# One 512-column product per high weight tile in the gate and up projections of a streaming encoder

## The chip, the core and the metric

The kernel runs on one core of a Trainium2 chip. The core's engines work side by side and meet at semaphores only: TensorE (PE in the profile, its weight loads PEld), VectorE (DVE), ScalarE (ACT), GpSimd (POOL) and SyncE (SP), which issues the loads. The metric is the time of one execution on the device in microseconds (us), as the median of several runs.

## The reference

Two layers run over a sequence of 256 tokens with 1024 features. Each layer is a gated feed-forward half step, a mixing step with three groups of heads, and a second gated feed-forward half step, each followed by a layer norm. The change is in the feed-forward part, of which there are four:

```
def swiglu(x, w_gu, w_down):
    gate, up = jnp.split(x @ w_gu, 2, axis=-1)
    return (jax.nn.silu(gate) * up) @ w_down

x = layer_norm(ALPHA * x + 0.5 * swiglu(x, ffn1_w_gu[l], ffn1_w_down[l]), ln1_g[l], ln1_b[l])
...
x = layer_norm(ALPHA * x + 0.5 * swiglu(x, ffn2_w_gu[l], ffn2_w_down[l]), ln3_g[l], ln3_b[l])
```

`w_gu` is 1024 by 5632 (2816 gate columns, then 2816 up columns), `w_down` 2816 by 1024, all float32.

## The kernel before

**Parts.** Every float32 operand of a large product is split in two: a high part rounded to the format that TensorE multiplies in one pass (fp32r), and a low part, the difference. A product is the sum of three: high by high, high by low, low by high. ScalarE writes the high part of a weight piece (`split_from`, L232) and VectorE the low part (L233), both in pieces of 128x512. The tokens `x` stand as two blocks of 128 tokens; `make_xT` transposes and splits them into the tiles `xh` and `xl`, each [128, 2 blocks, 4 k, 128 tokens], two pairs of them for the 8 slices of 128 features (`k`).

**Units.** A stage is a list of units of 128x1024 weight values. `load` brings a unit's raw weights into one of 5 buffers, `split` makes its two parts in one of 7 pairs of buffers (`wh`, `wl`), and `job` issues its products. `prepare` keeps up to 7 units split ahead of the products, and 5 loaded ahead of the splits. The instructions of an engine run in the order in which the builder's scheduler lays them down.

**Gate and up.** The 2816 columns are cut into 11 chunks of 256, each with its 256 gate columns and 256 up columns. The first 2 chunks of a feed-forward part are done block by block, because the second block's tokens arrive later. The other 9 (the ones with `both` set, 36 units) take both blocks at once, with the weights as the stationary operand and 256 token columns moving. A unit of these holds 2 slices `k` of all 512 columns of its chunk, so a chunk has 4 units and each unit 4 tiles of 128 columns:

```
for n, (a, x) in enumerate(((wh[:, s], xh), (wh[:, s], xl), (wl[:, s], xh))):
    self.nc.tensor.matmul(
        o, lhsT=a, rhs=x, start=k == 0 and n == 0 and i % 2 == 0, stop=end and n == 2,
```

That is three products of 256 columns for each tile and `k` (L295), added up in one half of a PSUM bank; the moving operand takes 128 columns from each block, in two pieces 512 values apart. A chunk uses two of the four banks of the pool `ps`. When it is done, `after_gu2` takes SiLU of the gate half on ScalarE (L447), multiplies by the up half on VectorE (L448), and splits the result into `hT`, the stationary operand of the down projection.

**Down.** The 22 units of `w_down` follow, per block, with `hT` as the stationary operand and 512 weight columns moving (`mm3`, L221, L222, L228, tile `po`). The input projection of the mixing step (`win`) uses the same code as gate and up for seven of its groups, with three products of 256 columns.

Of the kernel before, what the change touches and what calls it, by code (L numbers as in the profile page):

```python
# [11 lines left out]
F32R = mybir.dt.float32r  # L12
AF = mybir.ActivationFunctionType
# [4 lines left out]
P = 128  # L18
SEQ = 256
D = 1024  # L20
DFF = 2816
# [9 lines left out]
TSC = 2  # L31
# [60 lines left out]
class Kernel:  # L92
    def __init__(self, ctx, tc, a, out):
        self.tc, self.nc, self.a, self.out = tc, tc.nc, a, out
        pool = lambda name, bufs, **kw: ctx.enter_context(tc.tile_pool(name=name, bufs=bufs, **kw))
        self.const = pool("const", 1)
        self.raw_p = pool("raw", NRAW)
        self.wh_p = pool("wh", NW)
        self.wl_p = pool("wl", NW)
        self.xt_p = pool("xt", 4)  # L100
        self.big_p = pool("big", NBIG)
        self.w_p = pool("w", NHALF)
        self.h_p = pool("h", NH)
        self.s_p = pool("s", NS)
        self.gb_p = pool("gb", 1)
        psum = dict(space=bass.MemoryType.PSUM)
        self.ps_p = pool("ps", 4, **psum)
        self.aux_p = pool("aux", 4, **psum)
        self.n = 0
# [165 lines left out]
    def job(self, u, b):  # L275


        wh, wl = u["wh"], u["wl"]
        if u["kind"] in ("gu", "win"):
            width, ks = u["width"], u["ks"]  # L280
            g = u["group"]
            if u["part"] == 0:
                g["ps", b] = [self.ps("ps") for _ in range(len(u["tiles"]) // 2 if u["both"] else 1)]
            banks = g["ps", b]
            last = u["part"] == KD // ks - 1
            if u["both"]:
                for i, c0 in enumerate(u["tiles"]):
                    o = banks[i // 2][:, 256 * (i % 2) : 256 * (i % 2) + 256]
                    for kk in range(ks):
                        k = u["part"] * ks + kk  # L290
                        xh, xl = (t[:, :, k % 4, :] for t in self.xT[k // 4])
                        s = slice(kk * width + c0, kk * width + c0 + P)
                        end = last and kk == ks - 1
                        for n, (a, x) in enumerate(((wh[:, s], xh), (wh[:, s], xl), (wl[:, s], xh))):
                            self.nc.tensor.matmul(  # L295
                                o, lhsT=a, rhs=x, start=k == 0 and n == 0 and i % 2 == 0, stop=end and n == 2,
                                skip_group_check=True,
                            )
                        self.clock += 3 * 256 / 2400
                    if i < len(u["tiles"]) - 1:  # L300
                        self.step()
                if last:
                    self.spawn(u["then"](u, *banks))
                return
            ps = banks[0][:, :width]
            for kk in range(ks):
                k = u["part"] * ks + kk
                xh, xl = (t[:, b, k % 4, :] for t in self.xT[k // 4])
                s = slice(kk * width, (kk + 1) * width)
                self.mm3([ps], xh, xl, [(wh[:, s], wl[:, s])], k == 0, k == KD - 1)  # L310
            if last:
                self.spawn(u["then"](u, b, ps))
        else:
            if u["first"]:
                self.po[b] = [self.ps("po") for _ in range(2)]
            parts = self.hT if u["kind"] == "down" else self.mT
            t, kk = parts[u["k"] // 2, b], u["k"] % 2
            ws = [(wh[:, n * 512 : (n + 1) * 512], wl[:, n * 512 : (n + 1) * 512]) for n in range(2)]
            po = self.po[b]
            self.mm3(po, t[:, 0, kk, :], t[:, 1, kk, :], ws, u["first"], u["last"])  # L320
# [71 lines left out]

    def make_xT(self, b, seg):

        x = self.x[b]
        if b == 0:
            self.next_xT = []
        for n in range(2):
            ps = self.aux(b, "xps")
            self.transposes([x[:, (4 * n + k) * P : (4 * n + k + 1) * P] for k in range(4)], ps)  # L400
            if b == 0:
                self.next_xT.append(
                    [self.xt_p.tile([P, 2, 4, P], F32R, tag="xt", name=self.name(s)) for s in ("xh", "xl")]
                )
            hi, lo = self.next_xT[n]
            self.split_from(ps.rearrange("p (k t) -> p k t", k=4), hi[:, b], lo[:, b])
            yield 0.7
            self.xT = self.next_xT
            self.xready.add((seg, n, b))
# [28 lines left out]
        yield 0.8  # L438
        self.hT[u["c"], b] = g["hT"][:, b]

    def after_gu2(self, u, *banks):

        nc = self.nc
        tmp = self.big([2, 2, 256], "sghh")
        sg, hh = tmp[:, 0], tmp[:, 1]
        for j, ps in enumerate(banks):
            nc.scalar.activation(sg[:, j], ps[:, 0:256], AF.Silu)  # L447
            nc.vector.tensor_mul(hh[:, j], ps[:, 256:512], sg[:, j])  # L448
        t = self.big([2, 2, 2, P], "hT", F32R)
        self.split_from(hh.rearrange("p j (b t) -> p b j t", b=2), t[:, :, 0], t[:, :, 1])  # L450
        yield 1.0
        for b in range(2):
            self.hT[u["c"], b] = t[:, b]


    def after_win(self, u, *rest):
# [578 lines left out]
    def segments(self):  # L1035
        a = self.a
        segs = []

        def ffn(l, f):
            seg = len(segs)  # L1040
            last = l == L - 1 and f == 2
            units = []
            for c in range(NCH):
                group = {}
                both = c >= TSC
                for part in range(4):
                    units.append(
                        dict(kind="gu", w=a[f"ffn{f}_w_gu"][l], c=c, part=part, width=512, ks=2, group=group,
                             cols=((c * 256, 256), (DFF + c * 256, 256)), both=both, tiles=(0, 256, 128, 384),
                             then=self.after_gu2 if both else self.after_gu)  # L1050
                    )
# [146 lines left out]
```

## Time and profile before

| | us |
|---|---|
| median of 3 runs | 1108.71 (1108.1 to 1108.74) |
| the profiled execution | 1108.88 |
| its span, first to last instruction | 1107.1 |
| mean granted clock of TensorE in it | 0.992 of full speed |

| engine | busy, us | share of the span | instructions |
|---|---|---|---|
| PE | 1069.0 | 97% | 7549 |
| PEld | 961.6 | 87% | 7549 |
| DVE | 707.0 | 64% | 1351 |
| ACT | 555.8 | 50% | 1104 |
| POOL | 42.0 | 4% | 51 |

A matmul's duration in the profile includes its way through the array, during which the next one has begun; what a matmul costs in a row of them is the distance from its start to the next start. The chain of waits counts the time so. In it, the products of line L295 have 43% of the span, those of the down projection (`po`, L221, L222, L228) 21%.

### The profile page before, as it was taken

The numbers are of one execution on the slowest core, as the hardware profiler recorded it, in microseconds if no ns is written. First come the engines' busy times: TensorE is split into PE (matmuls) and PEld (weight loads), VectorE is DVE, ScalarE is ACT, GpSimd is POOL, SyncE is SP. The second block draws the span as 40 slices with busy tenths as digits, with TensorE's granted clock in tenths as the row PEclk, the third lists the DMA queues.
The fourth block names the chain that finished last, engine by engine and source line by source line (L and its number), as shares of the span: only waits on it lengthen the run. The fifth ranks groups of instructions, "written<-read, shape, count | busy, mean of one in ns | idle before, by whom it ended". The sixth has DMA issues, their size and how long they took to land.

```text
span 1107.1 us, 19618 instructions
## 1 busy us (share of the span) xinstructions
PE 1069.0 (97%) x7549; PEld 961.6 (87%) x7549; DVE 707.0 (64%) x1351; ACT 555.8 (50%) x1104; POOL 42.0 (4%) x51
## 2 busy tenths in 40 slices
PE   7999999999998999999999999999999999999996
PEld 5999988788987799998879999877888878999985
DVE  5665554896867865564585555467967687555544
ACT  6675543587433555454444555446764345454440
POOL 0000000001002000000000000000010110000001
PEclk9999999998999999999999999999999999999998
DMA  8876665661234666655476666646513348665541
GB/s 288 264 221 181 191 187 143 174 189 39 78 110 139 208 212 180 184 186 194 134 231 205 182 182 189 191 106 197 158 39 97 95 153 251 187 180 186 187 134 38
DMA packets 148629, 185.11 MB, mean 167 GB/s; under 512 B 15160, under 2 KB 128184, under 8 KB 148536
## 3 DMA queue, kind: packets, MB, share of 16 engines
q1 hardware_dynamic: 148536, 183.87, 54.3%
q8 instruction: 59, 0.97, 0.4%
q14 instruction: 34, 0.28, 0.1%
HBM read 182.78 MB, written 1.05 MB: 166 GB/s over the span
## 4 chain that ended last, share of the span: by engine, by line
PE 82%; DVE 8%; ACT 3%; DMA 2%; POOL 2%; issue 2%; SPq 0%; POOLq 0%; DVEq 0%; ACTq 0%
PE ps L295 43%; PE po L221 7%; PE po L222 7%; PE po L228 7%; PE ps L221 4%; PE ps L222 4%; PE ps L228 3%; DVE wl L233 3%; DMA raw<-in_ffn_w_gu_dram 1%; PE ups L349 1%; PE gps L349 1%; POOL rsq L390 1%; ACT wh L232 1%; DMA raw<-in_w_in_dram 1%; PE vnps L349 1%
## 5 line engine op out<-in xcount | busy, mean ns | idle before, releaser
L233 DVE TENSOR_TENSOR wl<-raw,wh 128x512 fp32r<-128x512 f32 (+1 forms) x672 | 434.3, 681 | 290.9 <-ACT wh L232 289.8
L232 ACT CAST wh<-raw 128x512 fp32r<-128x512 f32 (+1 forms) x672 | 384.4, 615 | 366.6 <-issue 137.0
L295 PE MATMUL ps<-xh,wl 128*128 128x256 f32 x1376 | 393.1, 286 | 0.0
L295 PE MATMUL ps<-xh,wh 128*128 128x256 f32 x1376 | 392.9, 286 | 0.0
L295 PE MATMUL ps<-xl,wh 128*128 128x256 f32 x1376 | 390.6, 284 | 0.0
L295 PEld LDWEIGHTS ps<-xh,wh 128*128 128x128 f32 x1376 | 265.4, 193 | 1.5 <-issue 1.1
L295 PEld LDWEIGHTS ps<-xh,wl 128*128 128x128 f32 x1376 | 265.3, 193 | 0.6 <-issue 0.5
L295 PEld LDWEIGHTS ps<-xl,wh 128*128 128x128 f32 x1376 | 265.2, 193 | 0.2
L221 PE MATMUL po<-wh,hT 128*128 128x512 f32 x352 | 137.7, 391 | 0.0
L222 PE MATMUL po<-wl,hT 128*128 128x512 f32 x352 | 137.1, 389 | 0.0
L228 PE MATMUL po<-wh,hT 128*128 128x512 f32 x336 | 103.5, 389 | 0.0
L221 PE MATMUL ps<-wh,xh 128*128 128x512 f32 (+2 forms) x256 | 97.2, 380 | 4.2 <-ACT wh L232 4.0
L222 PE MATMUL ps<-wl,xh 128*128 128x512 f32 (+2 forms) x256 | 94.6, 371 | 0.0
L228 PE MATMUL ps<-wh,xl 128*128 128x512 f32 (+2 forms) x224 | 83.6, 374 | 3.3 <-DVE xl L233 3.3
L221 PEld LDWEIGHTS po<-wh,hT 128*128 128x128 f32 x352 | 66.1, 188 | 14.4 <-DVE sghh L448 1.1
L222 PEld LDWEIGHTS po<-wl,hT 128*128 128x128 f32 x352 | 66.1, 188 | 13.3
L228 PEld LDWEIGHTS po<-wh,hT 128*128 128x128 f32 x336 | 63.1, 188 | 13.2
L221 PEld LDWEIGHTS ps<-wh,xh 128*128 128x128 f32 x256 | 48.5, 190 | 13.3 <-ACT wh L232 4.9
L222 PEld LDWEIGHTS ps<-wl,xh 128*128 128x128 f32 x256 | 48.6, 190 | 8.3 <-DVE wl L233 0.4
L228 PEld LDWEIGHTS ps<-wh,xl 128*128 128x128 f32 x224 | 42.4, 190 | 11.1 <-DVE xl L233 4.2
L388 POOL TENSOR_SCALAR rs<-mv 128x1 f32<-128x1 f32 x12 | 6.3, 527 | 804.1 <-DVE mv L372 804.1
L447 ACT ACTIVATE sghh<-ps 128x256 f32<-128x256 f32 x72 | 27.4, 382 | 12.7 <-PE ps L295 12.5
(231 smaller groups left out, 903.7 us busy)
## 6 DMA issues: line engine op xcount, KB each, us to landing
raw<-in_ffn_w_gu_dram SPq DMA_DIRECT2D x352, 256.0 KB, 3.5
raw<-in_ffn_w_down_dram SPq DMA_DIRECT2D x88, 512.0 KB, 3.5
raw<-in_w_in_dram SPq DMA_DIRECT2D x40, 512.0 KB, 3.9
raw<-in_w_out_dram SPq DMA_DIRECT2D x16, 512.0 KB, 3.3
raw<-in_w_in_dram SPq DMA_DIRECT2D x24, 256.0 KB, 3.6
g<-in_ln_g_dram SPq DMA_DIRECT2D x6, 512.0 KB, 4.9
b<-in_ln_b_dram SPq DMA_DIRECT2D x6, 512.0 KB, 5.7
x<-in_x_dram SPq DMA_DIRECT2D x4, 256.0 KB, 3.0
```

Source lines behind the costliest of these rows:

```text
L221: mm(p, lhsT=xh, rhs=wh, start=start, stop=False)
L222: mm(p, lhsT=xh, rhs=wl, start=False, stop=False)
L228: mm(p, lhsT=xl, rhs=wh, start=False, stop=False)
L232: self.nc.scalar.copy(hi, src)
L233: self.nc.vector.tensor_tensor(lo, src, hi.bitcast(F32), op=ALU.subtract)
L295: self.nc.tensor.matmul(o, lhsT=a, rhs=x, start=k == 0 and n == 0 and i % 2 == 0, stop=end and n == 2, skip_group_check=True,)
L349: self.nc.tensor.matmul(out, lhsT=lhsT, rhs=rhs, start=start, stop=stop)
L388: nc.gpsimd.tensor_scalar(t, ap, mul, add, op0=ALU.mult, op1=ALU.add)
L390: nc.gpsimd.tensor_tensor(r, t, self.neghalf[:, :n], op=ALU.pow)
L447: nc.scalar.activation(sg[:, j], ps[:, 0:256], AF.Silu)
```

## The change

**Products.** For each tile of 128 weight columns and each `k`, the two products with the high weight part become one of 512 columns, whose moving operand is high and low part of both blocks side by side. It fills a whole PSUM bank: columns 0 to 255 get high by high, columns 256 to 511 high by low. The product with the low weight part (256 columns, high tokens) is added into columns 0 to 255. So two matmuls stand where three stood, with the same number of columns.

**Tokens' tile.** `xh` and `xl` become one tile `xT` of [128, 4 k, 2 parts, 2 blocks, 128 tokens], so that the 512 columns of a `k` lie in one piece, and the 256 of its high part too. The pool holds 2 such tiles in place of 4 of half the size.

**Units.** Since a tile now needs a whole bank, the 9 chunks are worked off in halves `j` of 128 gate and 128 up columns, two banks each. A unit holds 4 slices `k` of one half, so a half has 2 units; its loads bring runs of 128 values (512 bytes) where they brought runs of 256 (1 KB). The number of units, loads and splits is the same.

**After the products.** `after_gu2` runs once for each half. ScalarE copies the upper 256 columns of a bank, VectorE adds the lower 256 to them, for gate and for up; then SiLU, product and split follow, each over 256 columns.

The input projection's groups keep three products of 256 columns; they read `xT`.

```
-                    o = banks[i // 2][:, 256 * (i % 2) : 256 * (i % 2) + 256]
                     for kk in range(ks):
                         k = u["part"] * ks + kk
-                        xh, xl = (t[:, :, k % 4, :] for t in self.xT[k // 4])
+                        x = self.xT[k // 4][:, k % 4].rearrange("p a b t -> p a (b t)")
...
-                        for n, (a, x) in enumerate(((wh[:, s], xh), (wh[:, s], xl), (wl[:, s], xh))):
+                        if len(banks) == 2:
+                            o, first = banks[i][:, 0:256], k == 0
+                            mms = [(banks[i], wh[:, s], x.rearrange("p a t -> p (a t)")), (o, wl[:, s], x[:, 0])]
+                        else:
+                            o, first = banks[0][:, 256 * i : 256 * i + 256], k == 0 and i == 0
+                            mms = [(o, wh[:, s], x[:, 0]), (o, wh[:, s], x[:, 1]), (o, wl[:, s], x[:, 0])]
+                        for n, (to, a, r) in enumerate(mms):
...
+                self.next_xT.append(self.xt_p.tile([P, 4, 2, 2, P], F32R, tag="xt", name=self.name("xT")))
...
-    def after_gu2(self, u, *banks):
-        tmp = self.big([2, 2, 256], "sghh")
-        sg, hh = tmp[:, 0], tmp[:, 1]
-        for j, ps in enumerate(banks):
-            nc.scalar.activation(sg[:, j], ps[:, 0:256], AF.Silu)
-            nc.vector.tensor_mul(hh[:, j], ps[:, 256:512], sg[:, j])
-        t = self.big([2, 2, 2, P], "hT", F32R)
-        self.split_from(hh.rearrange("p j (b t) -> p b j t", b=2), t[:, :, 0], t[:, :, 1])
+    def after_gu2(self, u, gate, up):
+        g = u["group"]["chunk"]
+        if "hT" not in g:
+            g["hT"] = self.big([2, 2, 2, P], "hT", F32R)
+        t = g["hT"]
+        a, hh = self.h(0, [256], "ga"), self.h(0, [256], "hh")
+        nc.scalar.copy(a, gate[:, 256:512])
+        nc.vector.tensor_add(a, gate[:, 0:256], a)
+        nc.scalar.copy(hh, up[:, 256:512])
+        nc.vector.tensor_add(hh, up[:, 0:256], hh)
+        nc.scalar.activation(a, a, AF.Silu)
+        nc.vector.tensor_mul(hh, hh, a)
+        j = u["j"]
+        self.split_from(hh.rearrange("p (b t) -> p b t", b=2), t[:, :, 0, j], t[:, :, 1, j])
...
+                for j in range(2):
+                    half, c0 = dict(chunk=group), c * 256 + j * P
+                    for part in range(2):
+                        units.append(
+                            dict(kind="gu", w=a[f"ffn{f}_w_gu"][l], c=c, j=j, part=part, width=256, ks=4, group=half,
+                                 cols=((c0, P), (DFF + c0, P)), both=True, tiles=(0, P), then=self.after_gu2)
+                        )
```

On PE, in the gate and up stage of the second feed-forward part, this stands before where one unit ends and the next begins (`ps` are the banks, `wh` and `wl` the parts of a unit's weights, `xh` and `xl` those of the tokens):

```order
L295 MATMUL ps_784_5195<-xh_623_4053,wh_759_5002 128x256
L295 MATMUL ps_784_5195<-xl_624_4054,wh_759_5002 128x256
L295 MATMUL ps_784_5195<-xh_623_4053,wl_760_5003 128x256
L295 MATMUL ps_783_5194<-xh_633_4092,wh_764_5043 128x256
L295 MATMUL ps_783_5194<-xl_634_4093,wh_764_5043 128x256
L295 MATMUL ps_783_5194<-xh_633_4092,wl_765_5044 128x256
```

And this stands there now, at a unit's beginning, at the change from its gate to its up tile, and at the next unit's beginning:

```order
L301 MATMUL ps_852_4933<-xT_673_3934,wh_823_4764 128x512
L301 MATMUL ps_852_4933<-xT_673_3934,wl_824_4765 128x256
...
L301 MATMUL ps_853_4934<-xT_673_3934,wh_823_4764 128x512
L301 MATMUL ps_853_4934<-xT_673_3934,wl_824_4765 128x256
...
L301 MATMUL ps_863_4994<-xT_664_3896,wh_828_4799 128x512
L301 MATMUL ps_863_4994<-xT_664_3896,wl_829_4800 128x256
```

Rows that repeat are left out: each pair stands four times in a row, once for each `k` of the unit. Outside the 36 units of each gate and up stage, PE's order is the same as before.

On ACT, the stretch around the end of a chunk before (`raw` are the loaded weights):

```order
L232 CAST wh_823_5560<-raw_806_5396 128x512 x2
L447 ACTIVATE sghh_826_5592<-ps_815_5470 128x256
L232 CAST wh_828_5600<-raw_809_5428 128x512
L447 ACTIVATE sghh_826_5592<-ps_816_5471 128x256
L232 CAST wh_828_5600<-raw_809_5428 128x512
L232 CAST hT_827_5597<-sghh_826_5592 128x2x256
```

And around the end of a half now, up to the next one:

```order
L454 COPY ga_837_4852<-ps_831_4808 128x256
L458 ACTIVATE ga_837_4852<-ga_837_4852 128x256
L232 CAST wh_839_4862<-raw_814_4707 128x512
L456 COPY hh_838_4853<-ps_832_4809 128x256
L232 CAST wh_839_4862<-raw_814_4707 128x512
L232 CAST hT_836_4851<-hh_838_4853 128x2x128
L232 CAST wh_844_4889<-raw_820_4743 128x512 x2
L454 COPY ga_847_4914<-ps_842_4871 128x256
```

The group of a chunk's end is repeated for each half, with two copies more, and its SiLU now reads what VectorE has added.

On DVE, the same stretch now (before, two products L448, a split of `hT` and the splits `wl` stood there for a chunk):

```order
L455 TENSOR_TENSOR ga_837_4852<-ps_831_4808,ga_837_4852 128x256
L233 TENSOR_TENSOR wl_840_4863<-raw_814_4707,wh_839_4862 128x512
L457 TENSOR_TENSOR hh_838_4853<-ps_832_4809,hh_838_4853 128x256
L233 TENSOR_TENSOR wl_840_4863<-raw_814_4707,wh_839_4862 128x512
L459 TENSOR_TENSOR hh_838_4853<-hh_838_4853,ga_837_4852 128x256
L233 TENSOR_TENSOR hT_836_4851<-hh_838_4853,hT_836_4851 128x2x128
L233 TENSOR_TENSOR wl_845_4890<-raw_820_4743,wh_844_4889 128x512 x2
L455 TENSOR_TENSOR ga_847_4914<-ps_842_4871,ga_847_4914 128x256
```

Two additions are new for each half; the product and the split of `hT` come once for each half, with 256 columns.

## Rows read from the trace of the kernel before

**Rows 1.** The page's busy times by engine and TensorE's granted clock in 40 slices

```profile
PE 1069.0 (97%) x7549; PEld 961.6 (87%) x7549; DVE 707.0 (64%) x1351; ACT 555.8 (50%) x1104; POOL 42.0 (4%) x51
PEclk9999999998999999999999999999999999999998
```

**Rows 2.** The chain of waits, gate and up stages: start us, us, what

```profile
39.69 38.15 PE ps L295 x318
77.94 61.91 PE ps L295 x516
393.42 100.07 PE ps L295 x834
```

**Rows 3.** Busy times in stretches: gate and up, down, loads with 512-byte runs

```profile
core 0: us, PE busy (x) PEld busy (x) DVE busy (x) ACT busy (x) POOL busy (x), PEclk, DMA share, GB/s
394.00:493.00 99.00, 99.00 (x828) 99.00 (x827) 56.54 (x95) 49.42 (x93) 0.00 (x0) 1.00 0.61 186
500.00:540.00 40.00, 40.00 (x179) 33.10 (x178) 17.96 (x28) 15.22 (x28) 0.00 (x0) 1.00 0.58 187
200.00:207.00 7.00, 6.04 (x34) 4.89 (x32) 7.00 (x16) 1.22 (x3) 1.22 (x2) 1.00 0.97 252
```

**Rows 4.** PE in order of time, down projection: start us, us, what

```profile
496.22 0.39 PE L221 MATMUL po<-wh,hT 128*128 128x512 f32 x1
...
496.90 0.39 PE L222 MATMUL po<-wl,hT 128*128 128x512 f32 x1
497.13 0.39 PE L228 MATMUL po<-wh,hT 128*128 128x512 f32 x1
```

**Rows 5.** PE in order of time, 256 moving columns in one piece

```profile
323.89 0.28 PE L222 MATMUL ps<-wl,xh 128*128 128x256 f32 x1
...
325.09 0.28 PE L228 MATMUL ps<-wh,xl 128*128 128x256 f32 x1
```

**Rows 6.** Groups of ACT: xcount | busy us, mean ns | idle before

```profile
L232 ACT CAST wh<-raw 128x512 fp32r<-128x512 f32 x656 | 378.5, 620 | 362.6 <-issue 137.0 <-PE po L228 107.1 <-PE ps L295 92.7
L447 ACT ACTIVATE sghh<-ps 128x256 f32<-128x256 f32 x72 | 27.4, 382 | 12.7 <-PE ps L295 12.5
L232 ACT CAST hT<-hTps 128x256 fp32r<-128x256 f32 x16 | 5.9, 366 | 0.4 <-PE hTps L237 0.4
L1003 ACT COPY do<-dops 128x256 f32<-128x256 f32 x4 | 1.4, 356 | 0.0
```

**Rows 7.** Groups of DVE by shape

```profile
L233 DVE TENSOR_TENSOR wl<-raw,wh 128x512 fp32r<-128x512 f32 x656 | 428.3, 687 | 290.7 <-ACT wh L232 289.8
L448 DVE TENSOR_TENSOR sghh<-ps,sghh 128x256 f32<-128x256 f32 x72 | 30.1, 420 | 1.2 <-ACT sghh L447 0.9
```

**Rows 8.** ACT in order of time at the end of a chunk

```profile
447.37 0.62 ACT L232 CAST wh<-raw 128x512 fp32r<-128x512 f32 x1 [0.98 <-PE ps L295]
447.90 0.38 ACT L447 ACTIVATE sghh<-ps 128x256 f32<-128x256 f32 x1
448.17 0.61 ACT L232 CAST wh<-raw 128x512 fp32r<-128x512 f32 x1
449.08 0.62 ACT L232 CAST hT<-sghh 128x512 fp32r<-128x512 f32 x1 [0.30 <-DVE sghh L448]
```

**Rows 9.** DVE in order of time, the same stretch

```profile
448.02 0.69 DVE L233 TENSOR_TENSOR wl<-raw,wh 128x512 fp32r<-128x512 f32 x1 [1.18 <-ACT wh L232]
448.63 0.42 DVE L448 TENSOR_TENSOR sghh<-ps,sghh 128x256 f32<-128x256 f32 x1
448.97 0.68 DVE L233 TENSOR_TENSOR wl<-raw,wh 128x512 fp32r<-128x512 f32 x1
449.74 0.69 DVE L233 TENSOR_TENSOR hT<-sghh,hT 128x512 fp32r<-128x512 f32 x1
```

**Rows 10.** The page's loads by line: xcount, KB each, median us to landing

```profile
raw<-in_ffn_w_gu_dram SPq DMA_DIRECT2D x352, 256.0 KB, 3.5
```

More of the change, by code (lines that the diff above doesn't have):

```diff
@@ L99, in __init__ @@
         self.wl_p = pool("wl", NW)
-        self.xt_p = pool("xt", 4)
+        self.xt_p = pool("xt", 2)
         self.big_p = pool("big", NBIG)
@@ L282, in job @@
             if u["part"] == 0:
-                g["ps", b] = [self.ps("ps") for _ in range(len(u["tiles"]) // 2 if u["both"] else 1)]
+                g["ps", b] = [self.ps("ps") for _ in range(2 if u["kind"] == "gu" and u["both"] else 1)]
             banks = g["ps", b]
@@ L287, in job @@
                 for i, c0 in enumerate(u["tiles"]):
-                    o = banks[i // 2][:, 256 * (i % 2) : 256 * (i % 2) + 256]
                     for kk in range(ks):
                         k = u["part"] * ks + kk
-                        xh, xl = (t[:, :, k % 4, :] for t in self.xT[k // 4])
+                        x = self.xT[k // 4][:, k % 4].rearrange("p a b t -> p a (b t)")
                         s = slice(kk * width + c0, kk * width + c0 + P)
                         end = last and kk == ks - 1
-                        for n, (a, x) in enumerate(((wh[:, s], xh), (wh[:, s], xl), (wl[:, s], xh))):
+                        if len(banks) == 2:
[5 more added lines that the diff above has]
+                        for n, (to, a, r) in enumerate(mms):
                             self.nc.tensor.matmul(
-                                o, lhsT=a, rhs=x, start=k == 0 and n == 0 and i % 2 == 0, stop=end and n == 2,
+                                to, lhsT=a, rhs=r, start=first and n == 0, stop=end and n == len(mms) - 1,
                                 skip_group_check=True,
@@ L307, in job @@
                 k = u["part"] * ks + kk
-                xh, xl = (t[:, b, k % 4, :] for t in self.xT[k // 4])
+                xh, xl = (self.xT[k // 4][:, k % 4, part, b, :] for part in range(2))
                 s = slice(kk * width, (kk + 1) * width)
@@ L401, in make_xT @@
             if b == 0:
[L402 to L406, printed above, removed]
+                self.next_xT.append(self.xt_p.tile([P, 4, 2, 2, P], F32R, tag="xt", name=self.name("xT")))
+            t = self.next_xT[n]
+            self.split_from(ps.rearrange("p (k t) -> p k t", k=4), t[:, :, 0, b], t[:, :, 1, b])
             yield 0.7
@@ L439, in after_gu @@
         self.hT[u["c"], b] = g["hT"][:, b]
-    def after_gu2(self, u, *banks):
+    def after_gu2(self, u, gate, up):
         nc = self.nc
-        tmp = self.big([2, 2, 256], "sghh")
-        sg, hh = tmp[:, 0], tmp[:, 1]
-        for j, ps in enumerate(banks):
-            nc.scalar.activation(sg[:, j], ps[:, 0:256], AF.Silu)
-            nc.vector.tensor_mul(hh[:, j], ps[:, 256:512], sg[:, j])
-        t = self.big([2, 2, 2, P], "hT", F32R)
-        self.split_from(hh.rearrange("p j (b t) -> p b j t", b=2), t[:, :, 0], t[:, :, 1])
+        g = u["group"]["chunk"]
[11 more added lines that the diff above has]
+        self.split_from(hh.rearrange("p (b t) -> p b t", b=2), t[:, :, 0, j], t[:, :, 1, j])
         yield 1.0
-        for b in range(2):
-            self.hT[u["c"], b] = t[:, b]
+        if j == 1:
+            for b in range(2):
+                self.hT[u["c"], b] = t[:, b]
     def after_win(self, u, *rest):
@@ L1044, in ffn @@
                 group = {}
[L1045 to L1051, printed above, removed]
+                if c < TSC:
+                    for part in range(4):
+                        units.append(
+                            dict(kind="gu", w=a[f"ffn{f}_w_gu"][l], c=c, part=part, width=512, ks=2, group=group,
+                                 cols=((c * 256, 256), (DFF + c * 256, 256)), both=False, then=self.after_gu)
+                        )
+                    continue
+                for j in range(2):
+                    half, c0 = dict(chunk=group), c * 256 + j * P
+                    for part in range(2):
+                        units.append(
+                            dict(kind="gu", w=a[f"ffn{f}_w_gu"][l], c=c, j=j, part=part, width=256, ks=4, group=half,
+                                 cols=((c0, P), (DFF + c0, P)), both=True, tiles=(0, P), then=self.after_gu2)
+                        )
             for k in range(2 * NCH):
```

## The prediction

> **What bounds the kernel now.** I read the busy times by engine first: PE is busy for 97% of the span, DVE for 64%, ACT for 50%, and TensorE's granted clock is full in all slices but one or two [rows 1]. A busy PE can still be waiting inside its queue, so the chain of waits decides. There the gate and up products of both blocks stand as single pieces of PE work that nothing else breaks: 834 matmuls in 100.07 us in the second feed-forward part [rows 2]. In the third and fourth parts the same row comes with the same numbers; in the first part a transpose cuts it into pieces of 318 and 516 [rows 2]. 30 matmuls more stand ahead of each, so a stage is 864 matmuls, 36 units of 24. The reader is to see three things there: the stage waits for no engine, the cost is 100.07 / 834 = 0.120 us for a matmul of 256 columns, and what is cut from PE's row there shortens the kernel, as long as ACT, DVE and the loads keep pace. In such a stage DVE is busy for 56.54 of 99 us and ACT for 49.42, and the loads take 0.61 of the DMA engines' time [rows 3].
>
> **The price of a matmul by its width.** The change keeps the number of columns and cuts the number of matmuls, so the question is what a matmul of 512 columns costs. The down projection has them in a row: from 496.22 to 497.13 there are four distances, 0.91 / 4 = 0.228 us [rows 4]. Over 40 us of it, 179 matmuls were under way [rows 3]; the first may have begun up to 0.39 us ahead of the window, so (40 + 0.39) / 179 = 0.226. I take 0.227. Two matmuls of 256 columns cost 0.240. So 0.013 us of each matmul doesn't hang on its columns, and that is what a merged pair saves.
>
> The Trainium skill prices this lower: "TensorE: Matmul & The Clock Gate", section "Back-to-back issue gap", gives N / 2.4 GHz plus about 2.5 ns at the full clock. By it a merged pair would save 2.5 ns, the change 1152 × 0.0025 = 2.9 us, and the kernel would come to 1105.8. The trace disagrees, with 0.120 and 0.227 us where that rule has 0.109 and 0.216.
>
> **Part by part.**
>
> Products. Each of the 36 units has 8 pairs of a weight tile and a `k`; with four stages that is 1152 pairs. Before: 3 × 0.120 = 0.360 us. Now: 0.227 + 0.120 = 0.347. The sum is 1152 × 0.013 = 15.0 us, 3.7 in each stage. The bounds: 0.226 and 0.228 for the wide matmul give 16.1 and 13.8.
>
> Tokens in one piece. Before, the 256 columns come in two pieces. The nearest row with 256 moving columns in one piece is a group of the mixing stage, where weights move: ten distances from 323.89 to 325.09, again 0.120 [rows 5]. So I count nothing for it, here and for the seven groups of the input projection. The starts are rounded to 0.01 us, so those ten distances can hide 0.001 us each, to either side: 1.8 us over the input projection's 672 products and the 1152 narrow ones, which is the bound.
>
> Work after the products. For a half ACT now has two copies from PSUM (like the 356 ns copy of 256 columns), a SiLU (like 382), a split of 256 columns (366) and 4 splits of 512 (620): 0.71 + 0.38 + 0.37 + 2.48 = 3.94 us [rows 6]. DVE has two additions, a product and a split of 256 columns (like 420) and 4 splits of 512 (687): 1.68 + 2.75 = 4.43 us [rows 7]. PE needs 16 × 0.347 = 5.55 us for a half. So each engine fits by itself, and its time is hidden by PE's row. But they now hand work to each other more often, and that chain is the critical part of this forecast.
>
> The chain of a half, in the order in which the instructions stand: addition for the gate (DVE), SiLU, split, on ACT; then on DVE low part, addition for up, low part, product; then on ACT the split of `hT` and a split; on DVE two low parts, and the next half's addition. From the rows at a chunk's end [rows 8, 9] I take these distances: a DVE operation of 256 columns and the hand-over to ACT 0.45 (448.63 to 449.08); on ACT 0.27 from an operation of 256 columns to the next (447.90 to 448.17); a split on ACT and the hand-over to DVE 0.66 (0.62 and the 0.04 that lie between 449.70 and 449.74); on DVE 0.61 from an operation of 512 columns to the next (448.02 to 448.63), 0.34 from one of 256 (448.63 to 448.97). The sum is 0.45 + 0.27 + 0.66 + 0.61 + 0.34 + 0.61 + 0.45 + 0.27 + 0.66 + 0.61 + 0.61 = 5.54 us, against PE's 5.55. The chain just fits, with no room. What saves it is the lead: up to 7 units are split ahead of PE, 7 × 2.78 = 19.4 us, and after the stage PE's down units cost 12 × 0.227 = 2.7 us against 2 × 0.69 us of splits on DVE, so the lead is made up there. I take 0, and bound it below by 0 and above by the rival's price.
>
> What speaks against the distances that I take is the Trainium skill, "VectorE: DVE Perf Modes", section "The DRAIN you can't avoid": the next operation doesn't start until the pipeline is empty. By that rule DVE's operations would not overlap, and the chain would be longer than PE's 5.55 us. The trace shows them 0.61 us apart where one takes 0.69 [rows 9], so I hold to the overlap; the rule is the case of the first rival.
>
> Waits for banks. A half's first matmul needs the banks of the half before the last. Behind the last matmul of a half come copy and addition, and a split or two that stand between them in the queues: about 2 us, and the next half's 5.55 lie between. At the end of the stage the down projection's second block takes the last half's banks after 1.4 us; before, the second product L448 stood there at the same place behind a split of ACT and one of DVE, and the addition takes as long as it did. Nothing is added.
>
> Loads. A unit's 524,288 bytes are now needed every 2.78 us, 189 GB/s, in runs of 512 bytes. The loads with such runs, in the input projection, came at 252 GB/s with 0.97 of the engines' time [rows 3]. So the share goes from 0.61 to 0.73, and the cover is the five raw buffers, 13.9 us, against 3.5 us to landing [rows 10]. If a unit took longer than 2.78 us, which needs a rate under 189, the stage would be bound by the loads; nothing in the rows comes near it.
>
> The profiled execution took 1108.88 us, 0.17 above the median of 1108.71; less 15.0 it gives 1093.9, and from the median 1093.7.
>
> **Rivals.**
>
> First, the chain of ACT and DVE becomes the bound, on the slower side. If operations did not overlap at all, the durations of [rows 6, 7] in place of the distances make it 0.45 + 0.38 + 0.66 + 0.69 + 0.42 + 0.69 + 0.45 + 0.37 + 0.66 + 0.69 + 0.69 = 6.15 us, 0.60 over PE's. That is 10.8 us over a stage's 18 halves, 43 us over four, less 15: 1137. Half of it, a chain of 5.85, gives 1093.7 + 22 = 1115. It decides from the point where the excess is no longer covered by the lead; 0.21 us for a half uncovered eats the whole gain. For it: the sum of 5.54 has no margin, and each half crosses between the engines four times. Against it: the lead of 19.4 us is more than the 10.8.
>
> Second, the 512 columns of tokens cost as much as two matmuls of 256, 0.240, because the 0.013 belong to the columns that are read and written, not to the matmul. Then nothing is saved: 1108.7. For it: no row of before has tokens as 512 moving columns. Against it: moving weights lie in the same memory, in the same format, and cost 0.227.
>
> Third, a part of the chain's excess shows, at the start of the down projection, where the lead is needed: 0.1 us for a half, 1.8 for a stage, 7 in all, 1101.
>
> **Chances.** The forecast has 0.80, with its own range of 1092 to 1096 (the bounds of the wide matmul, and what the pieces may give). The first rival has 0.06, the second 0.04, the third 0.07, and 0.03 stay for a time below 1092. Differences under 0.2% (2.2 us) can't be told from no change in this kernel. So: faster 0.90, same 0.04, slower 0.06. The range goes from 1091 to 1100; 0.15 are outside.
>
> **What would show it.** Right: in the chain of waits the gate and up stages are single pieces of some 556 matmuls (576 less those ahead of the transposes) in about 96 us; the wide matmul's next start comes after 0.227, the narrow one's after 0.120; ACT and DVE still wait for PE in that stage. Wrong in the first and third rival's way: the chain goes over DVE's low parts or the SiLU within a gate and up stage, or PE waits there for `wl` or at the first units of the down projection. Wrong in the second: distances of 0.240. Wrong in the loads: SP's loads land later than 13 us after their issue, or ACT's splits wait for a load. A gain outside the four stages, or one of over 17 us, would mean that I have missed a term.

## The result and the profile after

The changed kernel takes 1094.4 us (median of 4 runs, 1093.8 to 1096.02) where the kernel before takes 1108.72 (4 runs, 1108.1 to 1109.51): a ratio of 0.9875, 95% interval 0.9862 to 0.9887. The forecast was 1093.7. The profiled execution took 1094.49 us, its span 1092.7, which is 14.4 less than before.

The page of the changed kernel answers to [rows 1, 10]; in the third row, a group of TensorE, the number behind the second bar is PE's idle time before it and what ended it:

```profile
PE 1052.6 (96%) x6397; PEld 896.7 (82%) x6397; DVE 759.1 (69%) x1531; ACT 600.2 (55%) x1284; POOL 42.0 (4%) x51
...
PEclk9999999999999999999999999999999999999999
...
L221 PE MATMUL po<-wh,hT 128*128 128x512 f32 x352 | 137.7, 391 | 0.8 <-DVE hh L457 0.8
...
raw<-in_ffn_w_gu_dram SPq DMA_DIRECT2D x352, 256.0 KB, 3.5
```

PE has 1152 instructions fewer, DVE and ACT have the 180 more that the sums and the halves bring, and loads with runs of 512 bytes land as fast as those of 1 KB did. New is the 0.8 us for which PE waits at the down projection. The chain of waits answers to [rows 2] (start us, us, what):

```profile
40.86 41.61 PE ps L301 x240
82.58 43.01 PE ps L301 x248
130.08 1.09 DVE wl L233 x2
135.66 1.06 DVE wl L233 x2
...
386.90 4.23 PE ps L301 x24
391.36 95.69 PE ps L301 x552
```

The last row comes alike in the third and fourth parts. 552 products are 276 pairs: 95.69 / 276 = 0.3467 us for a pair, where three products took 0.360. From its first product to the first of the down projection a gate and up stage took 103.98, 103.88, 103.88 and 103.89 us, and takes 100.27 and three times 100.14: 14.9 us less in all. The rest of the span adds 0.5: the first loads and splits took 0.5 us longer (the first stage began at 36.24 us, before at 35.71; this differs between runs of one program, and a later trace of the changed kernel has 35.25), the first down stage 0.9 and all others together 0.2 longer, and the two stages of the input projection 0.5 and 0.6 shorter. In the first part the chain leaves PE 11 us before the stage ends and goes over DVE's low parts: that is the wait at the down projection, below.

Single products in PE's order of time, to be held against [rows 4, 5]:

```profile
450.13 0.39 PE L301 MATMUL ps<-xT,wh 128*128 128x512 f32 x1
450.36 0.28 PE L301 MATMUL ps<-xT,wl 128*128 128x256 f32 x1
450.48 0.39 PE L301 MATMUL ps<-xT,wh 128*128 128x512 f32 x1
```

From start to start the wide product takes 0.230 us and the narrow one 0.117. The stretches answer to [rows 3] (gate and up; the second row is the low level of TensorE's clock, 0.50 of 2.4 GHz, in the first mixing part; the second fence has such stretches of the kernel before, in its two mixing parts):

```profile
core 0: us, PE busy (x) PEld busy (x) DVE busy (x) ACT busy (x) POOL busy (x), PEclk, DMA share, GB/s
393.00:489.00 96.00, 96.00 (x552) 84.33 (x552) 69.86 (x139) 61.49 (x139) 0.00 (x0) 1.00 0.65 192
264.80:268.00 3.20, 3.20 (x13) 2.62 (x13) 0.19 (x2) 0.72 (x2) 2.90 (x1) 0.50 0.00 0
```

```profile
268.00:274.60 6.60, 5.73 (x25) 4.72 (x23) 4.40 (x14) 1.07 (x2) 2.13 (x1) 0.50 0.00 0
...
817.60:820.60 3.00, 3.00 (x16) 3.00 (x15) 3.00 (x10) 1.19 (x3) 0.00 (x0) 0.50 0.00 0
```

PE stays busy for the whole stretch, the loads take 0.65 of the DMA engines. Before, 13 of the input projection's products in the first layer and 16 in the second began at the low level; after, two did in the first, and in the second the low level is missing. Ahead of the fall stood short products of the mixing part in the first layer, and in the second layer of before a pause of PE of 2.2 us. The 0.5 and 0.6 us of that projection lie there: its 256-column products still stand 0.120 us apart at the full clock. They are no gain of the change: in another trace of the same program the second projection took 72.04 us again, with such a stretch in it, and the first 71.42.

### The profile page after: what moved, and what is told of

The parts are those of the page before. It is cut to its first block, busy times and chain, and to the rows that moved or that the text cites. A ratio compares the mean times of both kernels' runs of the same rounds, so it can differ in the third digit from the quotient of the medians.

```text
span 1092.7 us, 17702 instructions
## 1 busy us (share of the span) xinstructions
PE 1052.6 (96%) x6397; PEld 896.7 (82%) x6397; DVE 759.1 (69%) x1531; ACT 600.2 (55%) x1284; POOL 42.0 (4%) x51
## 4 chain that ended last, share of the span: by engine, by line
PE 79%; DVE 11%; ACT 3%; DMA 3%; issue 2%; POOL 2%; SPq 0%; DVEq 0%; POOLq 0%; ACTq 0%
PE ps L301 39%; PE po L221 7%; PE po L222 7%; PE po L228 7%; DVE wl L233 4%; PE ps L221 4%; PE ps L222 4%; PE ps L228 3%; DMA raw<-in_ffn_w_gu_dram 2%; PE ups L355 1%; PE gps L355 1%; DMA raw<-in_w_in_dram 1%; ACT wh L232 1%; POOL rsq L396 1%; PE vnps L355 1%
## 5 line engine op out<-in xcount | busy, mean ns | idle before, releaser
L301 PE MATMUL ps<-xT,wh 128*128 128x512 f32 (+1 forms) x1600 | 484.8, 363 | 0.0
L301 PE MATMUL ps<-xT,wl 128*128 128x256 f32 x1376 | 388.4, 282 | 0.0
L301 PEld LDWEIGHTS ps<-xT,wh 128*128 128x128 f32 x1600 | 285.3, 188 | 48.6 <-issue 1.1
L301 PEld LDWEIGHTS ps<-xT,wl 128*128 128x128 f32 x1376 | 260.5, 189 | 0.7 <-issue 0.5
L221 PE MATMUL ps<-wh,xT 128*128 128x512 f32 (+2 forms) x256 | 97.1, 379 | 4.3 <-ACT wh L232 4.2
L222 PE MATMUL ps<-wl,xT 128*128 128x512 f32 (+2 forms) x256 | 94.6, 371 | 0.0
L228 PE MATMUL ps<-wh,xT 128*128 128x512 f32 (+2 forms) x224 | 83.6, 374 | 3.4 <-DVE xT L233 3.4
L221 PEld LDWEIGHTS po<-wh,hT 128*128 128x128 f32 x352 | 66.1, 188 | 15.7 <-DVE hh L457 2.2
L221 PEld LDWEIGHTS ps<-wh,xT 128*128 128x128 f32 x256 | 48.5, 190 | 13.6 <-ACT wh L232 5.0
L222 PEld LDWEIGHTS ps<-wl,xT 128*128 128x128 f32 x256 | 48.6, 190 | 8.3 <-DVE wl L233 0.6
L458 ACT ACTIVATE ga<-ga 128x256 f32<-128x256 f32 x72 | 30.1, 418 | 42.4 <-DVE ga L455 42.2
L228 PEld LDWEIGHTS ps<-wh,xT 128*128 128x128 f32 x224 | 42.4, 189 | 11.1 <-DVE xT L233 4.2
L233 DVE TENSOR_TENSOR hT<-hh,hT 128x256 fp32r<-128x256 f32 x72 | 30.5, 424 | 25.8 <-ACT hT L232 25.6
```

The costliest lines, as they stand in the source:

```text
L221: mm(p, lhsT=xh, rhs=wh, start=start, stop=False)
L222: mm(p, lhsT=xh, rhs=wl, start=False, stop=False)
L228: mm(p, lhsT=xl, rhs=wh, start=False, stop=False)
L233: self.nc.vector.tensor_tensor(lo, src, hi.bitcast(F32), op=ALU.subtract)
L301: self.nc.tensor.matmul(to, lhsT=a, rhs=r, start=first and n == 0, stop=end and n == len(mms) - 1, skip_group_check=True,)
L458: nc.scalar.activation(a, a, AF.Silu)
```

## The experiments

All are edits of the changed kernel. Times are medians of 4 to 10 runs with a ratio to the kernel before on the same chip; two are single runs.

**The wide product cut in two.**

```
-mms = [(banks[i], wh[:, s], x.rearrange("p a t -> p (a t)")), (o, wl[:, s], x[:, 0])]
+mms = [(o, wh[:, s], x[:, 0]), (banks[i][:, 256:512], wh[:, s], x[:, 1]), (o, wl[:, s], x[:, 0])]
```

> The changed kernel with the 512 column product cut back into two of 256 columns (high tokens into columns 0 to 255 of the bank, low tokens into columns 256 to 511); layout of the tokens, units, banks, sums and order of the work stay as changed. Theory (each matmul costs about 13 ns beyond its columns, and nothing else of the change gains): the 1152 matmuls put back cost 1152 x 0.013 = 15 us, so about 1109, distances of 0.117 to 0.120 us on PE. Rival (the gain comes from the layout of the tokens' tile or from the new units and order): about 1094 to 1097.

Measured: 1108.5 us, ratio 1.0002 (0.9992 to 1.0011). The chain of waits of this kernel:

```profile
394.39 99.35 PE ps L301 x828
```

99.35 / 828 = 0.120 us. Layout, halves, sums and loads are those of the change, and the whole gain is gone: it hangs on the number of products alone. The price of a product beyond its columns is shown. Every product of this kernel comes with a load of its stationary operand (6397 of each after the change), so the 0.013 us are the price of the two together; no run takes them apart.

**The tokens in pieces.**

```
-x = self.xT[k // 4][:, k % 4].rearrange("p a b t -> p a (b t)")
+x = self.xT[k // 4][:, :, :, k % 4]
...
-self.xt_p.tile([P, 4, 2, 2, P], F32R, ...)
+self.xt_p.tile([P, 2, 2, 4, P], F32R, ...)
```

> The changed kernel with the tokens' tile laid out as before (part, block, k, token), so that the 512 moving columns come in four pieces of 128, the 256 of the high part in two, in the input projection too. Theory (the price is one of the matmul, pieces cost little): 0.227 to 0.232 us for the wide and about 0.120 for the narrow product; the 1.7 ns per product by which the input projection got faster come back on 672 + 2 x 1152 products, at most 5 us: 1094 to 1099. Rival (only one piece makes 512 columns cheaper than two times 256): 0.240 for the wide product, 1108 to 1110.

Measured: 1094.67 us (1093.45 to 1097.99), ratio 0.9882 (0.9864 to 0.9899): as the change. Four pieces of 128 columns cost no more than one of 512. But its trace showed something else. In the chain of waits, the second and the third gate and up stage, the same instructions:

```profile
390.94 95.69 PE ps L301 x552
...
578.07 97.53 PE ps L301 x552
```

And in the third stage, PE in order of time:

```profile
600.17 0.40 PE L301 MATMUL ps<-xT,wh 128*128 128x512 f32 x1
600.41 0.28 PE L301 MATMUL ps<-xT,wl 128*128 128x256 f32 x1
600.52 0.40 PE L301 MATMUL ps<-xT,wh 128*128 128x512 f32 x1
600.75 0.28 PE L301 MATMUL ps<-xT,wl 128*128 128x256 f32 x1
600.87 0.40 PE L301 MATMUL ps<-xT,wh 128*128 128x512 f32 x1
```

Here three pairs take 241 + 120 + 233 + 117 + 236 + 113 = 1060 ns, 0.3533 for a pair, against 0.3467. The granted clock is full in both, and no engine is waited for. Each of these two stages keeps its beat from end to end.

**Without the sums.**

```
-nc.scalar.copy(a, gate[:, 256:512])
-nc.vector.tensor_add(a, gate[:, 0:256], a)
-nc.scalar.copy(hh, up[:, 256:512])
-nc.vector.tensor_add(hh, up[:, 0:256], hh)
-nc.scalar.activation(a, a, AF.Silu)
-nc.vector.tensor_mul(hh, hh, a)
+nc.scalar.activation(a, gate[:, 0:256], AF.Silu)
+nc.vector.tensor_mul(hh, up[:, 0:256], a)
```

> The changed kernel without the two copies and two additions of a half: the products of the low tokens are made, but left out of the sum, so SiLU and the product with the up half read columns 0 to 255 of the banks. The chain of ACT and DVE for a half gets shorter by about 1.9 us (two hand-overs less). Theory (the chain is hidden beside PE, but for the 1 us that PE waits for a bank in the first down stage): about 1093.4. Rival (the chain takes time from PE in all four stages, at banks or at the lead): 1090 or less.

Measured: 1094.44 us (1092.54 to 1097.9), ratio 0.9878 (0.9859 to 0.9897). From this kernel's page, the group that waited in the changed one:

```profile
L221 PE MATMUL po<-wh,hT 128*128 128x512 f32 x352 | 137.3, 390 | 0.0
```

The wait is gone, and the first down stage took 83.98 us in place of 85.13. Its second gate and up stage ran in the slow beat (97.53 us for 552 products), which took the microsecond back and more. Against the changed kernel, copies and additions so cost the path 1 us in the first part and about 0.2 us in each later down stage; the median can't show that much. That the microsecond isn't their price in every order of the queues, the next experiment shows.

**A longer chain: one, four, six and eight operations more on DVE for each half.** The first was

```
 nc.vector.tensor_mul(hh, hh, a)
+nc.vector.tensor_scalar(hh, hh, 1.0, None, op0=ALU.mult)
```

> The changed kernel with one more VectorE operation of 256 columns for each half (hh times 1.0, between the second addition and the product), in the chain of ACT and DVE: 5.58 us measured for a half become about 5.92 (0.34 more), against PE's 5.55. The excess is 0.37 x 18 = 6.7 us for a stage. Theory of the prediction (the lead of 7 units, 19.4 us, covers it): 1094 to 1096, and no new wait. Rival (the lead doesn't cover it, since the down projection's second block needs the banks of the last half some 1.4 us after the stage's end, and these come only when the chain has caught up): the excess less what the stage's start leaves free, 4 to 6 us for each stage, shows as a wait of the first products into those banks: 1110 to 1117.

Here the operation stands behind the product of gate and up, ahead of the split of `hT`, and not ahead of the product as the text has it; it is in the same chain either way.

Measured: 1093.97 us (1092.46 to 1098.8), ratio 0.9885 (0.9862 to 0.9908). It tells the theories apart badly, for the chain didn't get longer: the scheduler laid the queues in another order. DVE's first addition of a half, in the changed kernel:

```profile
430.79 0.42 DVE L455 TENSOR_TENSOR ga<-ps,ga 128x256 f32<-128x256 f32 x1
...
436.37 0.42 DVE L455 TENSOR_TENSOR ga<-ps,ga 128x256 f32<-128x256 f32 x1
...
441.95 0.42 DVE L455 TENSOR_TENSOR ga<-ps,ga 128x256 f32<-128x256 f32 x1
```

and with one operation more:

```profile
429.49 0.42 DVE L455 TENSOR_TENSOR ga<-ps,ga 128x256 f32<-128x256 f32 x1
434.81 0.42 DVE L455 TENSOR_TENSOR ga<-ps,ga 128x256 f32<-128x256 f32 x1
440.59 0.42 DVE L455 TENSOR_TENSOR ga<-ps,ga 128x256 f32<-128x256 f32 x1
```

5.58 us in the one, 5.32 and 5.78 in turn in the other, 5.55 on average, which is PE's pace. In this order PE didn't wait at the first down stage either (84.08 us, where the changed kernel took 85.13), though all copies and additions are there and DVE has more to do: the last addition ended 1.76 us behind the first product of the down projection, where it ended 2.80 us behind it in the changed kernel. So the operations were made four:

```
+for _ in range(4):
+    nc.vector.tensor_tensor(hh, hh, hh, op=ALU.max)
```

> The changed kernel with four more VectorE operations of 256 columns for each half (hh = max(hh, hh), which leaves the values as they are), between the second addition and the product. Distances of VectorE without them are 4 x 0.61 + 4 x 0.34 = 3.8 us for a half when it never waits; the four add 0.34 to 0.45 each, 1.4 to 1.8, and the chain with its hand-overs goes from 5.58 to 6.4 or 7.2 us if the order of the queues doesn't hide them, against PE's 5.55. With x us of excess for a half: theory of the prediction (the lead of 7 split units, 19.4 us, covers a stage): no cost up to x = 1.08, so 1094 to 1096 for all but the upper end. Rival (queues are in a fixed order, so copies and additions fall behind with the splits, and a bank has only 5.55 - 2 = 3.5 us to spare): 18x - 3.5 for a stage, for x = 0.9 12.7 in each of four, 1145; PE then waits inside the gate and up stage for an addition.

Measured: 1094.76 us (1092.39 to 1095.59), ratio 0.9869 (0.9853 to 0.9886). A stretch of its second gate and up stage, the additions there, and the split of `hT`:

```profile
424.00:446.00 22.00, 22.00 (x129) 19.38 (x128) 21.26 (x48) 14.39 (x32) 0.00 (x0) 1.00 0.66 189
```

```profile
432.34 0.42 DVE L455 TENSOR_TENSOR ga<-ps,ga 128x256 f32<-128x256 f32 x1
432.90 0.43 DVE L233 TENSOR_TENSOR hT<-hh,hT 128x256 fp32r<-128x256 f32 x1
...
438.24 0.42 DVE L455 TENSOR_TENSOR ga<-ps,ga 128x256 f32<-128x256 f32 x1
```

DVE is busy for 21.26 of 22 us and still keeps PE's pace: the next half's addition now stands ahead of this half's split of `hT`, so one half's hand-overs lie under another half's work. The four gate and up stages take what they took; at the first down stage PE waited 1.2 us for banks (0.7 and 0.5), where it had waited 0.8. Inside a stage only DVE's own busy time is left as a bound, and the next two, with six and eight in place of four, go beyond it, each in a single run:

> As the kernel with four more VectorE operations for each half, but with six. There, VectorE was busy for 21.26 of 22 us in the second gate and up stage and kept PE's pace (11.09 us for two halves, so 5.55 each); two more operations of 0.34 to 0.45 us from start to start bring a half to 6.2 to 6.4 us, an excess of 0.65 to 0.85, 11.7 to 15.3 us over a stage's 18 halves. Theory of the prediction (the lead of 7 split units, 19.4 us, covers it): stages of 100.14 us, and no more than the 1 to 2 us of bank waits that the first down stage has now in the others: 1094 to 1100. Rival (a bank has only some 3.5 us to spare, then PE waits for the additions): 8 to 12 us for each stage, 1127 to 1143.

> As before with eight more operations for each half: 7.0 to 7.2 us of VectorE for a half, an excess of 1.45 to 1.65, 26 to 30 us over a stage. Theory of the prediction (19.4 us of lead): 7 to 10 us of each stage show, 1122 to 1134. Rival (3.5 us to spare): 23 to 26 us of each stage show, 1186 to 1198.

Measured: 1097.06 and 1132.66 us. With six, the stages of the second to fourth parts are whole and unchanged; the first shows where PE waited (engine line <- what it waited for: us in total, times, longest):

```profile
394.40 95.69 PE ps L301 x552
```

```profile
PEld ps L301 <- DVE lam L213: 2.0, 1, 2.0
PE ps L301 <- DVE lam L213: 1.7, 1, 1.7
```

DVE needs 5.86 us for a half there (four halves from 459.35 to 482.78 us). That is 0.31 over PE, less than expected, 5.5 us for a stage, and all of it is covered: by the rival 2 us of each stage would show. DVE was busy there for 88.63 of 89 us. The first stage took 104.42 us, 4.15 longer; some 2.8 of that lie at three waits, of which the one shown is the longest (`lam` is one of the set-up operations that stand in DVE's queue in the first part), and most of the rest comes from the slow beat, in which PE's row went on from about 86 us. With eight, PE runs 24 products ahead of the transposes and the 215 of this row, then waits (chain of waits; then PE in order of time; then what was waited for between 399 and 509 us):

```profile
404.11 37.34 PE ps L301 x215
```

```profile
451.03 0.47 PE L301 MATMUL ps<-xT,wh 128*128 128x512 f32 x1 [1.15 <-DVE ga L455]
```

```profile
PEld ps L301 <- ACT hh L456: 6.3, 4, 1.6
...
PE ps L301 <- DVE ga L455: 5.3, 4, 1.5
...
PE ps L301 <- ACT wh L232: 1.3, 1, 1.3
```

Stages two to four take 108.66, 108.57 and 108.56 us, 8.4 to 8.5 more than with four. In the second, PE stood still for 6.6 us of that, in five waits; the rest goes with its new starts and with the slow beat. DVE needs 12.85 us for two halves (from one first addition to the next but one), 0.87 over PE for each; over 18 halves that is 15.7, of which 7.2 were covered. Neither theory had the size: the cover is about 7 us, not 19.4 and not 3.5. It ends as the rival said, mostly at the banks, which come free with the copy `hh` and the addition `ga`; in the second stage only one wait of five is for a split. That the time lies in the range of the lead's sum says little: there the later stages were to show 7 to 10 us for an excess of 26 to 30, and the first, which has less cover, took 114.02 us, 13.75 longer.

This trace shows one thing more of the two beats: behind a wait the row may go on in the other. In the second stage 12 pairs take 4.160 us ahead of the first wait, 4.240 behind the waits that end at 451.03, 476.74, 489.59 and 502.44 us, and 4.160 again behind the one that ends at 463.88.

**The second block of down later.**

```
-closing = lambda at, hi: min(LAG, max(1, LAG - (hi - at[0]) // 2))
+closing = lambda at, hi: min(LAG, max(2, LAG - (hi - at[0]) // 2))
```

> The changed kernel with the down projection's first block kept two units ahead of the second at the stage's start instead of one, so that the banks of the last half are needed 1.36 us later. Theory (PE's wait of 1.0 us in the first down stage is for the bank of the last half): that wait goes, 1093.4; nothing changes in the other three. Rival (it is a wait for something else, or moves to the next unit): 1094.4.

Measured: 1096.25 us (1095.86 to 1097.0), ratio 0.9891 (0.9876 to 0.9906). The start of the first down stage, in the changed kernel:

```profile
138.12 0.40 PE L222 MATMUL po<-wl,hT 128*128 128x512 f32 x1
139.36 0.50 PE L221 MATMUL po<-wh,hT 128*128 128x512 f32 x1 [0.84 <-DVE hh L457]
```

and with the second block later:

```profile
137.92 0.40 PE L222 MATMUL po<-wl,hT 128*128 128x512 f32 x1
138.15 0.39 PE L221 MATMUL po<-wh,hT 128*128 128x512 f32 x1
```

The theory holds for the wait: the stage went from 85.13 to 84.00 us. The time went up all the same: in both layers TensorE's clock fell at the end of the mixing part, where it had stayed full in the changed kernel, and the stages there took 95.23 and 95.49 us where they took 93.68 and 93.67:

```profile
342.00:345.40 3.40, 3.40 (x11) 2.62 (x12) 3.17 (x6) 1.09 (x2) 0.00 (x0) 0.50 0.42 144
```

Ahead of this stretch PE had stood still for 2.91 us, from 338.22 to 341.13, waiting for DVE's `y`, and as long in the second layer; in the changed kernel these two waits are 1.6 us each. The edited line also sets the order of the output projection at the end of the mixing part, so the edit was not confined to the down stages, and what was expected of it ("nothing changes in the other three") left that out. That the longer waits brought the clock down fits the trace but was not tried apart. It is no better version.

**Another order of the products**, wide, wide, narrow, narrow:

```
+todo += [(n, first, end, len(mms), m) for n, m in enumerate(mms)]
+if len(banks) == 2:
+    if kk % 2 == 0:
+        continue
+    todo.sort(key=lambda z: z[0])
...
```

> The changed kernel with another order of the same products: for two slices k at a time the two wide products, then the two narrow ones. The trace shows two beats in the stages, each kept for a whole stage: 0.3467 us for a pair (230 + 117 ns) and 0.3533 (six products of 241, 120, 233, 117, 236 and 113 ns), 1.84 us apart over 276 pairs; which one comes differs from stage to stage and from one kernel to the next. Theory (a fixed price for each product, whatever its neighbour): 2 x 0.347 = 0.694 for two pairs, 1094. Rival (a beat of wide against narrow products adds to the price): 0.227 and 0.117 in rows of equal ones, 0.688, 3.5 us less, and no second beat: 1090 to 1092.

Measured: 1095.29 us (1095.13 to 1095.99), ratio 0.9883 (0.9868 to 0.9897). The chain of waits, second and third stage:

```profile
390.75 96.14 PE ps L307 x552
...
578.28 96.15 PE ps L307 x552
```

0.3483 us for a pair, in every stage. The rival's gain isn't there: the price is that of the product, not of a change of width. A second beat didn't show, and its four runs lie within 0.9 us. That this order has none isn't shown: the one trace has three whole stages, and in the order of the changed kernel, too, only 4 of the 24 whole stages traced ran in the slow beat.

**The change once more.**

> The changed kernel once more, unchanged. Theory (the spread of its runs comes from stages that run in the slower of two beats, 1.84 us each): times in steps of some 1.8 us above the lowest, from 1092.5 to 1098, and a stage of 101.98 in place of 100.14 us wherever the trace is of a longer run. Rival (the spread is the clock's or the loads'): all four stages alike in the trace, and the time lost elsewhere.

Measured: 1095.76 us (1093.59 to 1096.01), ratio 0.9881 (0.9866 to 0.9896). The third stage took 95.69 us for its 552 products; the fourth:

```profile
927.34 97.53 PE ps L301 x552
```

The same program, and now that stage runs in the slow beat. That a stage's beat is a matter of the execution is shown; that it makes up a good part of the runs' spread is likely (1.84 us for a stage), but only the traced ones can be read, and these two differ elsewhere too: the first stage began 1.0 us earlier here, and the second layer's input projection took 0.6 longer. What sets the beat stays open. In the second to fourth parts the slow stages are those in which PE's first distance behind the transposes ahead of the stage is 318 or 319 ns, in the others it is 314 or 315; but the first part has 317 or 318 there and ran in the fast beat.

## Why the prediction was right, step by step

**Price of a product: right.** 0.360 to 0.347 forecast, 0.360 to 0.3467 measured, and cutting the product in two brought all of it back. (By the formula of the Trainium skill, "TensorE: Matmul & The Clock Gate", section "Back-to-back issue gap", each product less would have given 2.5 ns; the runs show 13. The prediction took that formula as the rule for a row, but the section gives it for a product on its own and names another spacing for a row of weight loads and products, about 131 ns at 512 columns. The trace agrees with neither: 227 to 230 ns.) The parts were off by 3 ns each way (0.230 and 0.117 for 0.227 and 0.120), and the sum of them was not. In the slow beat a stage gains (0.360 - 0.3533) x 288 = 1.9 us in place of 3.7; the forecast had one price for every stage, so a run with one slow stage lies 1.84 us above it, within its range. All four stages of the profiled execution ran in the fast beat.

**Tokens in one piece, counted as 0: right.** In pieces the time is the same, and the input projection's products still take 0.120 us.

**The chain, 5.54 us "with no room": right in number, wrong in kind.** It measured 5.58. But it is the length of one order of the queues, not a bound: with four operations more, the scheduler's order still kept PE's pace. The bound is DVE's busy time, 4.04 us for a half (69.86 of 96 us; the forecast added up 4.43), against PE's 5.55. That operations of DVE overlap held: those of 512 columns still follow one another after 0.60 to 0.61 us where one takes 0.69. By the Trainium skill, "VectorE: DVE Perf Modes", section "The DRAIN you can't avoid", the next operation doesn't start until the pipeline is empty; the same section adds that one which isn't held starts earlier, which the prediction left out and the trace agrees with. The first rival rested on operations that don't overlap at all, and had less for it than its text says.

**The lead of 19.4 us as cover: mis-sized.** It was not needed in three of four parts. What covers in these is about 7 us, and it ends where the banks do. The third rival's sign, a chain over DVE's low parts and a wait in the first down units, did show, in one part of four and with 1.0 us.

**Waits for banks, "nothing is added": wrong by 1.0 us**, in the first down stage. The addition's own duration was compared, not what stands ahead of it. The last half's copy `hh` on ACT began at 138.16 us, 1.65 after the first product of the down projection (136.51), and the addition that frees the bank at 138.89:

```profile
138.16 0.36 ACT L456 COPY hh<-ps 128x256 f32<-128x256 f32 x1
138.89 0.42 DVE L457 TENSOR_TENSOR hh<-ps,hh 128x256 f32<-128x256 f32 x1
```

It ended 2.80 us behind that first product; in the other three parts it ended 1.82 or 1.83 behind it. In the first part the chain has fallen behind, because set-up operations stand in DVE's queue and wait there for ACT and for loads (DVE of the changed kernel in order of time):

```profile
58.63 0.17 DVE L202 TENSOR_SCALAR nA<-nA 128x12 f32<-128x12 f32 x1 [2.69 <-ACT nA L201]
63.02 0.20 DVE L203 TENSOR_SCALAR subw<-subw 128x64 f32<-128x64 f32 x1 [1.95 <-DMA subw<-in_da_subln_w_dram]
...
76.08 0.20 DVE L203 TENSOR_SCALAR subw<-subw 128x64 f32<-128x64 f32 x1 [3.10 <-DMA subw<-in_da_subln_w_dram]
```

That is 7.7 us of standing still, about the cover that the longer chains measured. That these operations are the cause was not tried apart, but four traces whose queues stand in the same order bear it out: with 7.15 us of these waits (the run that asks for the bank later) the addition ended 2.24 us behind the first product of the down projection, with 7.52 (the change once more) 2.60, with 7.74 (the changed kernel) 2.80, with 7.79 (the tokens in pieces) 2.85. That the wait is for that bank is shown by the run that asked for it later, and by the run without the sums, whose shorter chain took it away. The run with one operation more in the chain had no wait either, so the 1.0 us belong to the sums in this order of the queues.

**Loads: right that they don't bind, and the share was too high.** 0.65 of the DMA engines for 0.73 forecast, 3.5 us to landing, no wait.

The profiled execution was to take 1093.9 us and took 1094.49: 0.1 from the products, 0.9 from the bank, 0.5 from the start, 0.2 elsewhere, less 1.1 in the input projection. The 15 us of the products are the mechanism; that the rest came to 0.6 is partly luck, since the bank's 0.9 and the start's 0.5 were met by 1.1 of the clock, for which the forecast had no term.

## What to carry to other kernels

Count matmuls, not only columns: where the distance from start to start has a part that doesn't hang on the width, merging two products that share their stationary operand saves that part, and the row that prices it can come from another stage of the same trace. An adder chain across engines that "just fits" by adding up distances says little where a scheduler may overlap successive pieces: compare the busy time of each engine with PE's, and look for the cover in the part that has the least of it, here the first, with its set-up work.

## What the runs showed of the hardware

- A row of alternating 512 and 256 column products has two beats, 0.3467 and 0.3533 us for a pair at the full clock. In a stage without waits a row kept its beat (some 96 us); behind a wait it went on in the other in some cases. Rows of 256 alone (0.120) showed one in all eight stages traced, the order wide, wide, narrow, narrow (0.3483) one in a single trace.
- Four pieces of 128 moving columns, 2 KB apart in a partition, cost the same as one piece of 512: 95.69 us for 552 products in both.
- A DVE that was busy for 21.26 of 22 us, in another run for 88.63 of 89, didn't hold up PE within a stage; with eight operations more it was busy for all of 89.99 us, with 0.87 us more work for a half than PE, and PE waited.
